# State-space units 1 to 7: loads and output stores issued from POOL's queue in place of SyncE's

## The chip, the cores and the metric

The kernel runs on one core of a Trainium2 chip. The metric is device time in microseconds (us) for one execution; lower is better. Instructions go to engines that run side by side, each in its own order: TensorE (PE in the profile, with its weight loads as PEld), VectorE (DVE), ScalarE (ACT), GpSimd (POOL) and SyncE (SP). SP computes nothing: it issues DMA transfers. POOL can issue DMA transfers too, and computes as well.

## The reference

One layer of a hybrid block in float32: 2048 frames of width 1024. One RMSNorm feeds one input projection, whose columns are split between a state-space layer and chunked attention; both outputs are normalised, joined, projected and added to the input; a SwiGLU feed-forward part and a final RMSNorm follow.

```python
h = rmsnorm(x, norm_mix_g)
proj = h @ w_in
u_ssm, q, k, v = split(proj)                       # 512 columns each
y_ssm = s5_mixer(u_ssm, ...)                       # 32 groups of 16 channels, 64 complex states per group
y_att = chunked_attention(q, k, v, rel_bias)       # 8 heads, own 64-frame chunk and the 8 before it
x = x + concat(rmsnorm(y_ssm), rmsnorm(y_att)) @ w_out
x = x + (silu(h2 @ w_gate) * (h2 @ w_up)) @ w_down # h2 = rmsnorm(x)
return rmsnorm(x)

# inside s5_mixer, per group: bu = B_bar u;  s[t] = lam_bar * s[t-1] + bu[t];  y = Re(C s) + D u
```

## The kernel before

The state-space layer is computed in blocks of eight frames. A first phase writes the input of the layer, u, and three sets of matrices to DRAM: Bst (from the inputs of a block to the state at its end), Tm (from the inputs of a block to its own outputs) and Vm (from the state before a block to its outputs). The recurrence then runs over 256 blocks only.

The work of this layer is cut into eight units (`ssm_unit`, b = 0 to 7, four channel groups each). A unit

1. loads U (eight transfers, one per frame of the block, 16 partitions each), Bst (one), Tm (eight) and Vm (one): 18 transfers, in `load`;
2. multiplies U by Bst on PE (tile `pj`); ACT copies the result to X (line 588);
3. scans X over the blocks on POOL (lines 602 to 605, then the carries in lines 613 and 614);
4. shifts the scanned states by one block into XG, with four transfers from POOL's queue (line 636);
5. multiplies U by Tm and XG by Vm on PE; ACT copies the result to Y (line 646), and eight transfers store Y to DRAM, as `y` (line 649).

U, Bst, Tm and Vm have one buffer each, so a load of the next unit may only land when the matmuls of the unit before that read this buffer are done.

The units run inside the attention phase (`att_phase`). Attention is a list of 128 steps (four blocks of 512 queries, four pairs of heads, two heads, four parts), and units of other work are fed into these steps: the q/k projections, the v projections, the preparation of the next block's input and the eight state-space units, one after the other, each over 15 steps. A unit is a generator; at each step it is advanced so many times, and YL = 8 of these advances lie between the loads and the first matmul, YX = 8 between the XG transfers and the second matmuls.

PE's order is that of the program (every matmul of the attention phase is kept in program order). The order on ACT, DVE, POOL and SP is set by the scheduler when the program is built: by priority, that is place in the program, and by what it expects to be ready. On the chip each engine takes its own list in that order, and an instruction that waits holds all behind it. SP's list holds, beside the transfers of the state-space units: the weights of the projections (`w<-wss`, 1 MB each), their input (`xt`, `raw`), the relative-position bias (`nba`, `nbb`), keys kept from the block before (`k<-ks`, `ks<-k`), halves of q moved to other partitions (`q2h`, `q2l`) and the attention's output (`ya_s<-ya`). POOL's list holds, in this phase, the scans and the XG transfers alone.

Once the last unit is done, the mixing stage loads y (`yr<-y`) and the attention's output, and goes on to the gated unit and the output projection.

`k.ssm_eng`, which is passed to `ssm_unit` as `eng`, is POOL (`nc.gpsimd`).

Of the kernel before, what the change touches and what calls it, by code (L numbers as in the profile page):

```python
# [20 lines left out]
NG, CH, NS = 32, 16, 64  # L21
# [535 lines left out]
def ssm_unit(k, p, psum, S, b, eng):  # L557

    nc = k.nc
    F = GB * CH  # L560
    U = k.t(p, "U", [P, GB, NC])

    def load(out, in_):
        ins = nc.sync.dma_start(out, in_)
        if b == 0:
            k.tc.keep_in_program_order(ins)

    for j in range(L):
        load(U[j * CH : (j + 1) * CH].rearrange("c g (n t) -> c g n t", n=NSB), S["u"].rearrange("(c g) n j t -> c g n j t", c=CH)[:, GB * b : GB * b + GB, :, j])
    gs = slice(GB * b, GB * b + GB)  # L570
    bst = k.t(p, "Bst", [P, GB, P])
    load(bst[:].rearrange("p g m -> p (g m)"), S["bst"][b // 2][:, (b % 2) * GB * P : (b % 2 + 1) * GB * P])
    tm = k.t(p, "Tm", [P, GB, P])
    for i in range(L):
        load(tm[i * CH : (i + 1) * CH], S["kt"].rearrange("c g a m -> c g (a m)")[:, gs, P - CH * i : 2 * P - CH * i])
    vm = k.t(p, "Vm", [P, GB, P])
    load(vm[:], S["v"].rearrange("q g c n m -> (c n) (q g) m")[:, gs, CH:])
    for _ in range(YL):
        yield

    X = k.t(p, "X", [P, 2, GP, NC])
    for q in range(GP):
        ps = k.t(psum, "pj", [P, 2, NC], bufs=2)
        for g2 in range(2):
            k.ta.matmul(ps[:, g2, :], bst[:, 2 * q + g2, :], U[:, 2 * q + g2, :], start=True, stop=True)
        for g2 in range(2):
            for c in range(2):
                nc.scalar.copy(X[g2 * NS : (g2 + 1) * NS, c, q, :], ps[c * NS : (c + 1) * NS, g2, :])
        yield

    a8 = S["a8"]
    qs = slice(GP * b, GP * b + GP)
    Xk = X[:].rearrange("p r q (k s) -> p r q k s", s=8)
    Xe = Xk[:, :, :, :, 7].rearrange("p r q (a b) -> p r q a b", b=8)

    def step(dst, src, e, n):

        ar = a8[:, 0, qs, (0, 7, 15)[e]].unsqueeze(1).to_broadcast([P, 2, GP]).unsqueeze(3).to_broadcast([P, 2, GP, n])
        aw = S["sw"][:, e, :, qs].unsqueeze(3).to_broadcast([P, 2, GP, n])
        t = k.t(p, "st1", [P, 2, GP, NC // 8])  # L600
        t2 = k.t(p, "st2", [P, 2, GP, NC // 8])
        eng.tensor_tensor(t[:, :, :, :n], src, ar, op=ALU.mult)  # L602
        eng.tensor_tensor(t2[:, :, :, :n], src[:, ::-1], aw, op=ALU.mult)
        eng.tensor_tensor(dst, dst, t[:, :, :, :n], op=ALU.add)  # L604
        eng.tensor_tensor(dst, dst, t2[:, :, :, :n], op=ALU.add)  # L605

    def carry(dst, end, i0, n):

        for c in range(2):
            for e in range(2):  # L610
                t = k.t(p, "fx", [P, GP, NC // 8, 7])[:, :, :n]
                pw = a8[:, c if e == 0 else 1 - c, qs, i0 : i0 + 7].unsqueeze(2).to_broadcast([P, GP, n, 7])
                eng.tensor_tensor(t, end[:, e].unsqueeze(3).to_broadcast([P, GP, n, 7]), pw, op=ALU.mult)
                eng.tensor_tensor(dst[:, c], dst[:, c], t, op=ALU.subtract if e == 1 and c == 0 else ALU.add)
            yield

    for s in range(1, 8):
        step(Xk[:, :, :, :, s], Xk[:, :, :, :, s - 1], 0, NC // 8)
        yield
    for b_ in range(1, 8):  # L620
        step(Xe[:, :, :, :, b_], Xe[:, :, :, :, b_ - 1], 1, 4)
        yield
    for a in range(1, 4):
        step(Xe[:, :, :, a : a + 1, 7], Xe[:, :, :, a - 1 : a, 7], 2, 1)
        yield
    yield from carry(Xe[:, :, :, 1:, :7], Xe[:, :, :, :3, 7], 8, 3)
    yield from carry(Xk[:, :, :, 1:, :7], Xk[:, :, :, : NC // 8 - 1, 7], 0, NC // 8 - 1)

    if b == 0:
        k.XG = k.t(p, "XG", [P, GB, NC])  # L630
        nc.gpsimd.memset(k.XG[:, :, 0:1], 0.0)
    XG = k.XG
    XGv = XG[:].rearrange("p (q g) c -> p q g c", g=2)
    for g2 in range(2):
        for c in range(2):
            eng.dma_start(XGv[c * NS : (c + 1) * NS, :, g2, 1:], X[g2 * NS : (g2 + 1) * NS, c, :, : NC - 1])
    for _ in range(YX):
        yield
    Y = k.t(p, "X", [P, GB, NC])
    for q in range(GP):  # L640
        ps = k.t(psum, "pj", [P, 2, NC], bufs=2)
        for g2 in range(2):
            g = 2 * q + g2
            k.ta.matmul(ps[:, g2, :], tm[:, g, :], U[:, g, :], start=True, stop=False)
            k.ta.matmul(ps[:, g2, :], vm[:, g, :], XG[:, g, :], start=False, stop=True)
        nc.scalar.copy(Y[:, 2 * q : 2 * q + 2, :], ps[:])
        if q == GP - 1:
            for j in range(L):
                nc.sync.dma_start(S["y"][b * F : (b + 1) * F, j, :].rearrange("(g c) t -> c g t", c=CH), Y[j * CH : (j + 1) * CH])
        yield  # L650


# [25 lines left out]
def att_phase(k, ident, S, aw, x0, roots):  # L678

    tc, nc, io, pfs = k.tc, k.nc, k.io, k.pfs  # L680
    with ExitStack() as cx:
# [256 lines left out]
        for b in range(NG // GB):  # L938
            units.append(Unit(ssm_unit(k, sp, psum, S, b, k.ssm_eng), SSM_N, 2 + int(SW * b), 2 + int(SW * (b + 1)), light=SL))
# [757 lines left out]
```

## Time and profile before

| | us |
|---|---|
| median of 3 runs | 2290.89 (2288.25 to 2294.39) |
| the profiled execution | 2289.1 |
| its span, first to last instruction | 2287.1 |
| PE busy | 2171.6 |
| DVE busy | 1544.7 |
| ACT busy | 1000.6 |
| POOL busy | 348.7 |

The span runs from the first to the last instruction of the profiled execution. Busy times are sums over an engine's instructions; engines overlap, so they do not add up to the span. DMA transfers are not counted as busy on SP. On POOL their issue is. Where a row of the profile ends in `[1.45 <-DMA ...]`, the engine stood idle for 1.45 us before it, and the named transfer or instruction ended last of what it waited for; a name can be that of another transfer on the same semaphore. "Landing" is the time from the issue of a transfer to its completion.

The first state-space unit loads from 138 us of the span on; the last one stores y at 696 to 700 us.

### The profile page before, as it was taken

To read this page: it belongs to the slowest core of one execution; us is meant where nothing else is said; L and a number is where in the kernel's file an instruction comes from. 1 tells how busy PE (TensorE), PEld (TensorE's weight loads), DVE (VectorE), ACT (ScalarE), POOL (GpSimd) and SP (SyncE) were. 2 spreads that over 40 slices of the span, in tenths; PEclk is the share of its full clock that TensorE was granted. 3 is DMA by queue.
4 is the path that set the end of the run, shared out by engine and by line. 5 is a ranking of instruction groups with operands and counts; after the bars stand their busy time and mean duration, and the time that the engine had idled before them with its cause. 6 is when DMAs were issued, how large, how long until landed. Compare 5 with 4: busy or idle time off the path is not lost.

```text
span 2287.1 us, 30278 instructions
## 1 busy us (share of the span) xinstructions
PE 2171.6 (95%) x10632; PEld 1830.1 (80%) x10632; DVE 1544.7 (68%) x2695; ACT 1000.6 (44%) x1654; POOL 348.7 (15%) x813
## 2 busy tenths in 40 slices
PE   8988899999996899999999999999999989999997
PEld 6777688898985788878888887888888778888886
DVE  7755565555556766876776678666666477789776
ACT  6444555455557652343333335333333343344322
POOL 2245765455660000000000000000000000000000
PEclk9998999999998999999999999999999999999999
DMA  8767886666644534854465567555423297465552
GB/s 299 236 221 220 257 223 201 187 188 179 188 132 124 171 121 147 267 189 151 160 200 178 167 211 258 203 169 188 139 96 110 78 341 252 166 212 193 206 189 74
DMA packets 215256, 428.33 MB, mean 187 GB/s; under 512 B 38592, under 2 KB 61168, under 8 KB 208000
## 3 DMA queue, kind: packets, MB, share of 16 engines
q1 hardware_dynamic: 210368, 412.50, 55.3%
q0 software_dynamic: 4736, 13.91, 2.0%
q8 instruction: 83, 1.36, 0.2%
q14 instruction: 69, 0.57, 0.1%
HBM read 286.86 MB, written 129.00 MB: 182 GB/s over the span
## 4 chain that ended last, share of the span: by engine, by line
PE 80%; DVE 6%; DMA 4%; POOL 4%; issue 3%; ACT 1%; SPq 1%; DVEq 0%; POOLq 0%; ACTq 0%
PE X L79 20%; PE ps L79 19%; PE Y L79 10%; PE pf L79 9%; PE big L79 9%; PE W L79 5%; PE pj L79 4%; PE sc L79 2%; PE pt L82 2%; DMA xt<-in_xp 1%; DMA hd<-wc 1%; POOL X L605 1%; DVE lo L156 1%; POOL X L604 1%; POOL st L602 1%
## 5 line engine op out<-in xcount | busy, mean ns | idle before, releaser
L79 PE MATMUL X<-hi,c 128*128 128x512 f32 x1408 | 451.0, 391 | 6.9 <-DVE c L156 5.4
L79 PE MATMUL ps<-hd,hd 128*128 128x512 f32 (+1 forms) x1968 | 430.8, 381 | 6.1 <-ACT hd L156 4.5
L79 PEld LDWEIGHTS ps<-hd,hd 128*128 128x128 f32 x1968 | 358.0, 189 | 77.7 <-ACT hd L156 5.3
L79 PEld LDWEIGHTS X<-hi,c 128*128 128x128 f32 x1408 | 265.3, 189 | 63.4 <-DVE c L156 6.3
L79 PE MATMUL X<-lo,c 128*128 128x512 f32 x704 | 274.9, 391 | 0.0
L156 ACT CAST hd<-hd 128x1536 fp32r<-128x1536 f32 (+1 forms) x106 | 147.7, 1393 | 236.3 <-DMA hd<-hq 178.7
L79 PE MATMUL Y<-hi,c 128*128 128x512 f32 x704 | 224.7, 390 | 1.5 <-DVE u L1389 1.5
L156 DVE TENSOR_TENSOR hd<-hd 128x1536 fp32r<-128x1536 f32 (+1 forms) x106 | 174.4, 1646 | 29.1 <-ACT hd L156 28.4
L156 DVE TENSOR_TENSOR c<-S,c 128x512 fp32r<-128x512 f32 x176 | 121.0, 689 | 98.3 <-ACT c L156 98.0
L1385 ACT COPY u<-X 128x512 f32<-128x512 f32 x132 | 77.4, 587 | 200.7 <-PE X L79 200.7
L1513 DVE TENSOR_TENSOR acc<-acc,ps 128x512 f32<-128x512 f32 x196 | 130.9, 684 | 50.3 <-PE ps L79 47.8
L156 ACT CAST c<-S 128x512 fp32r<-128x512 f32 x176 | 109.4, 622 | 120.1 <-PE Y L79 61.6
L79 PE MATMUL pf<-hi,w 128*128 128x512 f32 x416 | 153.9, 422 | 8.4 <-ACT w L156 4.7
L79 PE MATMUL big<-m,woh 128*128 128x512 f32 x512 | 161.2, 396 | 0.0
L79 PEld LDWEIGHTS Y<-hi,c 128*128 128x128 f32 x704 | 132.5, 188 | 29.9 <-DVE u L1389 2.2
L79 PEld LDWEIGHTS X<-lo,c 128*128 128x128 f32 x704 | 132.8, 189 | 27.5
L156 ACT CAST c<-raw 128x512 fp32r<-128x512 f32 x132 | 82.3, 623 | 150.5 <-PE Y L79 68.5
L79 PE MATMUL Y<-lo,c 128*128 128x512 f32 x352 | 137.2, 390 | 0.0
L868 DVE TENSOR_TENSOR ptl<-pt,pth 128x640 fp32r<-128x640 f32 (+3 forms) x152 | 98.3, 647 | 47.5 <-ACT pth L867 45.9
L852 ACT ACTIVATE s<-s,mn 128x640 f32<-128x640 f32 (+4 forms) x128 | 98.0, 765 | 65.6 <-DVE mn L849 61.1
L867 ACT CAST pth<-pt 128x640 fp32r<-128x640 f32 (+3 forms) x152 | 83.8, 551 | 95.6 <-PE pt L82 91.5
L79 PE MATMUL W<-hi,c 128*128 128x512 f32 x352 | 115.5, 389 | 0.0
(441 smaller groups left out, 4169.9 us busy)
## 6 DMA issues: line engine op xcount, KB each, us to landing
w<-wss SPq DMA_DIRECT2D x36, 1024.0 KB, 6.0
hq<-g SPq DMA_DIRECT2D x140, 256.0 KB, 2.1
hd<-hq SPq DMA_DIRECT2D x42, 768.0 KB, 4.5
hd<-wc SPq DMA_DIRECT2D x42, 768.0 KB, 6.0
raw<-in_w_gate SPq DMA_DIRECT2D x44, 512.0 KB, 3.8
raw<-in_w_up SPq DMA_DIRECT2D x44, 512.0 KB, 4.3
wc<-px SPq DMA_DIRECT2D x66, 256.0 KB, 3.2
wss<-w SPq DMA_DIRECT2D x12, 1024.0 KB, 5.7
```

What stands on the lines that cost most here:

```text
L79: return self.tc.keep_in_program_order(self.tc.nc.tensor.matmul(*a, **b))
L82: return self.tc.keep_in_program_order(self.tc.nc.tensor.transpose(*a, **b))
L156: return nc.scalar.copy(hi, raw), nc.vector.tensor_tensor(lo, raw, f32(hi), op=ALU.subtract)
L602: eng.tensor_tensor(t[:, :, :, :n], src, ar, op=ALU.mult)
L604: eng.tensor_tensor(dst, dst, t[:, :, :, :n], op=ALU.add)
L605: eng.tensor_tensor(dst, dst, t2[:, :, :, :n], op=ALU.add)
L852: nc.scalar.activation(s[:, :nk], s[:, :nk], AF.Exp, bias=mn[:], scale=-1.0, accum_out=sums[sb, pr][:, hh, qp : qp + 1])
L867: nc.scalar.copy(pth[:, a:b, qp, :], pt[:, a:b, :])
L868: nc.vector.tensor_tensor(ptl[:, a:b, qp, :], pt[:, a:b, :], f32(pth[:, a:b, qp, :]), op=ALU.subtract)
L1385: nc.scalar.copy(u[:], ps[:])
L1513: V.tensor_tensor(a, a, ps[:], op=ALU.add)
```

## The change

In units 1 to 7 the 18 loads are issued from POOL's queue in place of SP's. In the first unit (b = 0) they stay on SP, kept in program order there as before. The eight stores of y are issued from POOL's queue in all eight units. Sizes, tiles and buffers are as before.

```diff
     def load(out, in_):
-        ins = nc.sync.dma_start(out, in_)
         if b == 0:
-            k.tc.keep_in_program_order(ins)
+            k.tc.keep_in_program_order(nc.sync.dma_start(out, in_))
+        else:
+            eng.dma_start(out, in_)
...
         if q == GP - 1:
             for j in range(L):
-                nc.sync.dma_start(S["y"][b * F : (b + 1) * F, j, :].rearrange("(g c) t -> c g t", c=CH), Y[j * CH : (j + 1) * CH])
+                eng.dma_start(S["y"][b * F : (b + 1) * F, j, :].rearrange("(g c) t -> c g t", c=CH), Y[j * CH : (j + 1) * CH])
```

## The prediction

> **What bounds the kernel now.** I read the page's table of engines first, then the waits, the timelines of the stretch in which the state-space units run (130 to 700 us of the span), and the rows of POOL's own DMAs.
>
> ```profile
> PE 2171.6 (95%) x10632; PEld 1830.1 (80%) x10632; DVE 1544.7 (68%) x2695; ACT 1000.6 (44%) x1654; POOL 348.7 (15%) x813
> ```
>
> TensorE is busy for 95% of the span, and its order is fixed, so the end moves only where PE stands still or where its clock drops. POOL has 85% idle. The change touches eight units of about 70 us each. The view of waits over 130 to 710 us (us in total, times, longest) gives the waits that belong to them, and the same view of SP's queue gives one more:
>
> ```profile
> POOL st L602 <- ACT X L588: 217.3, 8, 32.6
> PE pj L79 <- DMA Tm<-kts: 11.1, 4, 3.7
> PE pj L79 <- DMA XG<-X: 3.6, 2, 1.9
> SPq L649 <- ACT X L646: 16.3, 7, 6.1
> ```
>
> The first row is POOL between two units: it stands empty for 217.3/8 = 27 us each time, so there is room for issues. The second is what the change can win or enlarge: PE stands still for 11.1 us in four of the seven handovers from one unit to the next, because the loads of the next unit have not landed when its first matmuls (U by Bst, into pj) come up. The name Tm there is only that of another DMA on the same semaphore; the matmul reads U and Bst. PE's timeline at the seven handovers, units 1 to 7 in order (start, us, what, in brackets PE's idle time before it):
>
> ```profile
> 227.11 0.67 PE L79 MATMUL pj<-U,Bst 128*128 128x256 f32 x2 [1.45 <-DMA Tm<-kts]
> 300.02 1.35 PE L79 MATMUL pj<-U,Bst 128*128 128x256 f32 x5 [2.92 <-DMA Tm<-kts]
> 364.46 1.97 PE L79 MATMUL pj<-U,Bst 128*128 128x256 f32 x8 [3.00 <-DMA Tm<-kts]
> 441.04 1.24 PE L79 MATMUL pj<-U,Bst 128*128 128x256 f32 x5
> 504.94 1.89 PE L79 MATMUL pj<-U,Bst 128*128 128x256 f32 x8
> 575.05 1.89 PE L79 MATMUL pj<-U,Bst 128*128 128x256 f32 x8
> 642.56 1.88 PE L79 MATMUL pj<-U,Bst 128*128 128x256 f32 x5 [3.73 <-DMA Tm<-kts]
> ```
>
> PE was ready at start minus idle: 225.66, 297.10, 361.46, 441.04, 504.94, 575.05, 638.83. What starts each handover is ACT's second copy of Y; its rows for the same seven handovers:
>
> ```profile
> 215.86 0.58 ACT L646 COPY X<-pj 128x512 f32<-128x512 f32 x1
> 284.96 0.59 ACT L646 COPY X<-pj 128x512 f32<-128x512 f32 x1 [1.10 <-PE pj L79]
> 352.35 0.59 ACT L646 COPY X<-pj 128x512 f32<-128x512 f32 x1 [1.09 <-PE pj L79]
> 426.71 0.59 ACT L646 COPY X<-pj 128x512 f32<-128x512 f32 x1 [0.92 <-PE pj L79]
> 493.48 0.59 ACT L646 COPY X<-pj 128x512 f32<-128x512 f32 x1 [0.92 <-PE pj L79]
> 563.02 0.59 ACT L646 COPY X<-pj 128x512 f32<-128x512 f32 x1 [1.10 <-PE pj L79]
> 629.39 0.59 ACT L646 COPY X<-pj 128x512 f32<-128x512 f32 x1 [1.10 <-PE pj L79]
> ```
>
> The copies end at 216.44, 285.55, 352.94, 427.30, 494.07, 563.61 and 629.98. Then SP issues eight stores of y and eight loads of U, one behind the other. SP's timeline at units 1, 2, 3 and 7:
>
> ```profile
> 216.47 4.16 SPq L649 DMA_DIRECT2D y<-X  x8
> 220.72 3.81 SPq L564 DMA_DIRECT2D U<-u  x8
> ...
> 285.58 3.61 SPq L649 DMA_DIRECT2D y<-X  x8
> 291.21 0.34 SPq L695 DMA_DIRECT2D w<-wss  x1
> 291.59 3.53 SPq L564 DMA_DIRECT2D U<-u  x7
> ...
> 351.92 0.32 SPq L564 DMA_DIRECT2D U<-u  x1
> 352.96 4.96 SPq L649 DMA_DIRECT2D y<-X  x8
> 357.97 3.62 SPq L564 DMA_DIRECT2D U<-u  x7
> ...
> 632.08 3.94 SPq L649 DMA_DIRECT2D y<-X  x8
> 636.52 3.53 SPq L564 DMA_DIRECT2D U<-u  x7
> ```
>
> At units 1, 3 and 7 PE starts 2.58, 2.87 and 2.51 us after the last U issue ends (224.53, 361.59, 640.05). At unit 2 a 1 MB weight load stood ahead on SP: it held the queue from 289.19 to 291.21, and U landed only 4.9 us after its last issue (295.12). At unit 7 the queue was 2.1 us late (632.08 against 629.98). So on SP the chain is copy of Y, eight stores, eight loads, landing, and twice something foreign in between.
>
> **The change, part by part.**
>
> *Taken from SP.* For units 1 to 7 the 18 loads, and for all eight units the 8 stores: 7 x 18 + 8 x 8 = 190 issues. At unit 1 the sixteen that stand ahead of the matmul cost 224.53 - 216.47 = 8.06 us. SP is not on the path elsewhere in these stretches, so I count only what comes earlier through it: the weight load at unit 2 and the 2.1 us at unit 7. These leave the chain.
>
> *Put on POOL's queue.* POOL's present DMAs, by form (busy us, mean ns):
>
> ```profile
> L636 POOL DMA_DIRECT2D XG<-X x32 | 19.7, 616 | 2.4 <-POOL X L614 2.4
> L368 POOL DMA_DIRECT2D vs<-v x16 | 10.1, 636 | 10.8 <-DVE v L288 7.6 <-DVE ny L113 1.7 <-DVE nv L109 1.6
> L358 POOL DMA_DIRECT2D kts<-kt x4 | 2.2, 547 | 8.3 <-DVE kt L357 7.2 <-DVE nf L111 1.0
> ```
>
> A store of y and a load of Tm touch 16 partitions in 64 runs, and are nearest to the kts row (16 partitions, 64 KB): 0.55 us. A load of U has 256 runs like the vs row: 0.63 us. I take one U load ahead of the stores, as at 351.92 above (its buffer is free once the matmuls that read it end, some 1.4 us before the copy does). From the end of the copy to the end of the last U issue: 8 x 0.55 + 7 x 0.63 = 8.81 us. On SP it was 8.09, 9.57, 8.65 and 10.07 us at units 1, 2, 3 and 7.
>
> *Landing.* No row shows a load of this kind on POOL's queue. The tile views give the times from issue to landing (min/median/max), first of XG (POOL, 127.5 KB), then of U and of y (both SP, 64 KB):
>
> ```profile
> DMA to landing us min/median/max: 2.4/4.6/7.9
> DMA to landing us min/median/max: 2.2/3.0/7.5
> DMA to landing us min/median/max: 2.0/2.1/7.4
> ```
>
> At their shortest the two queues differ by 0.2 to 0.4 us, with twice the bytes on POOL's side; at their medians by 1.6. XG is issued among large weight loads, so I take the short end: 2.6 us after the last issue, as at units 1, 3 and 7. The long end, 1.6 more, goes into the range.
>
> *Stalls after.* Copy end + 8.81 + 2.6 gives landings at 227.85, 296.96, 364.35, 438.71, 505.48, 575.02 and 641.39. Against PE's ready times that leaves stalls of 2.2, 0, 2.9, 0, 0.5, 0 and 2.6 us: 8.2 in place of 1.45 + 2.92 + 3.00 + 3.73 = 11.1. Gain 2.9 us.
>
> *Clock.* Around the longest stall (unit 7) and after that of unit 3, the windows view (width, busy PE, PEld, DVE, ACT, POOL, granted clock, DMA share, GB/s):
>
> ```profile
> 643.00:647.00 4.00, 4.00 (x14) 3.40 (x13) 0.21 (x1) 2.68 (x8) 0.00 (x0) 0.57 0.53 136
> 365.00:369.00 4.00, 3.81 (x21) 3.27 (x20) 0.83 (x2) 3.24 (x9) 0.24 (x1) 1.00 0.77 224
> 575.00:645.00 70.00, 66.27 (x410) 60.25 (x410) 35.28 (x64) 37.05 (x75) 35.01 (x88) 0.99 0.63 180
> ```
>
> After 3.73 us of idle the granted clock was 0.57 for 4 us, after 3.00 us it stayed at 1.00. So a stall above some 3.0 to 3.7 us costs 4 x 0.43 = 1.7 us more, and at 2.6 us unit 7 saves it. The Trainium skill (TensorE: Matmul & The Clock Gate, Part 1) puts the idle window at about 3.4 us; these two rows agree with it.
>
> *POOL's own work behind the issues.* In POOL's order the 8 loads of Tm and one of Vm stand between U and the scan: 8 x 0.55 + 0.63 = 5.0 us, one more for Bst, 5.6. The scan cannot start before U has landed, the matmuls have run and ACT has copied eight times; at unit 3, ACT's timeline has
>
> ```profile
> 365.64 3.04 ACT L588 COPY X<-pj 64x256 f32<-64x256 f32 x8 [4.51 <-issue]
> ```
>
> which ends at 368.68, 4.2 us after PE's start at 364.46. With the landing of 2.6 that is 6.8 us against 5.6: hidden, with 1.2 us of cover. If the cover goes, each microsecond costs one at the units where PE already waits for XG (3.6 us in two waits above). A load of Bst, whose buffer is free early, may stand between two scan steps, 0.6 us; I count 1.5 us for two or three units. Who waits behind POOL's queue: only this kernel's scan; nothing else uses POOL here.
>
> *The last unit.* Its y goes to the mixing stage, which loads it after other transfers; with 8 x 0.55 in place of 3.6 us the store is under 1 us later, and I count nothing.
>
> Sum: -2.9 - 1.7 + 1.5 = -3.1 us. The profiled execution took 2289.1 us (span 2287.1), 1.8 below the median of 2290.9; less 3.1 it is 2286.0, and on the median's footing 2287.8. I forecast 2288 us, which is within 0.3% (6.9 us, about what a measurement of this kernel can tell from no change).
>
> **The rivals.**
>
> *POOL's issues are slow beside VectorE (slower).* DVE is busy for 35.28 of 70 us in the row above. If each of the sixteen issues ahead of the matmul waits for half of a DVE operation of 0.7 us at half occupancy, that is 16 x 0.35 x 0.5 = 2.8 us; the long landing alone is 1.6. With 1.6 to 2.8 us more at every handover the stalls become 3.8, 1.5, 4.5, 0, 2.1, 1.6, 4.2 = 17.7 up to 5.0, 2.7, 5.7, 0.5, 3.3, 2.8, 5.4 = 25.4; less 11.1, and with two to three more clock drops (3.4 to 5.1 us), the time is 10 to 19 us longer, with Bst's 1.5 some 2302 to 2312. It decides from 0.8 us per handover on, where unit 7 crosses the clock's limit again. For it speaks that no load of 256-byte runs was ever on this queue; against it, that the 32 XG issues in these same stretches took 0.587 to 0.694 us (mean 0.616, row above). The Trainium skill (SBUF — State Buffer, SBUF: two separate sides) warns of just this: POOL writes its descriptors through a port that some VectorE operations lock, with an issue of 620 ns becoming 3100 ns. The XG rows do not show it. Chance 0.31.
>
> *The queues come apart (faster).* If POOL gets more U loads out ahead of the stores, or its landing is as short as 2.4 us, every handover's stall goes: -11.1 - 1.7 = -12.8, some 2278; the attention's transfers, no longer behind 26 issues, can add to it. One stall that could go so stands in PE's timeline, where hi is made from a load on SP's queue:
>
> ```profile
> 252.30 0.50 PE L79 MATMUL pf<-hi,w 128*128 128x512 f32 x1 [3.15 <-ACT hi L728]
> ```
>
> With it 2275. Against it: POOL is no quicker per issue than SP. Chance 0.27.
>
> *The cover on POOL goes (slower by little).* If the 5.6 us of Tm, Vm and Bst outlast the 6.8, the scan starts 1 to 2 us late. XG is already awaited in two units; if it decides in three or four, that is 3 to 8 us on top of the forecast: 2291 to 2296. Chance 0.08.
>
> **How the numbers follow.** The forecast has 0.34; its own range is 2282 to 2295 (unit 2's landing of 4.9 us, one or no U load ahead). Of it 0.05 lies below -0.3% and 0.04 above +0.3%. The first rival gives 0.27 slower and 0.04 same, the second 0.25 faster and 0.02 same, the third 0.04 and 0.04. Together faster 0.30, same 0.35, slower 0.35. The range that leaves out some 2 in 10 runs from 2274 to 2310.
>
> **What would show it.** Right: POOL's rows have 190 more DMA issues of 0.53 to 0.65 us; POOL's wait for ACT's copy falls from 217 us by some 100; PE's wait before U by Bst is 7 to 10 us in total, none at unit 2; the clock row at unit 7 is 1.00. Wrong: POOL DMA rows of 1 us or more, U's landing above 4 us, waits before U by Bst of more than 15 us, or PE waiting for XG by more than 5 us. If all of these fit and the time is off by over 0.3%, then the order of SP's remaining transfers changed the attention's stalls, which I have not counted.

## The result, and the profile after

The changed kernel takes 2319.95 us in the median of four runs (2313.49 to 2325.72), against 2291.39 us for the kernel before in the runs beside it. The ratio is 1.0126 with a 95% interval of 1.0106 to 1.0146: 1.3% slower, 28.6 us. The forecast was 2288 us with a range of 2274 to 2310, so the time lies above the range, on the side of the first rival but beyond it. The profiled execution of after is the slowest of the four: 2325.72 us, span 2323.8 us, 36.7 us more than the span of before.

The page's table of engines, after:

```profile
PE 2186.9 (94%) x10632; PEld 1842.6 (79%) x10632; DVE 1546.9 (67%) x2695; ACT 999.4 (43%) x1654; POOL 450.0 (19%) x1003
```

POOL has its 190 more instructions, as the change says, and 101 us more of busy time. PE does the same 10,632 matmuls but is busy 15 us longer: the same work at a lower clock. The next view tells how much of the loss lies in the state-space stretch. It is the windows view between the same two matmuls of PE's fixed order, in before and then in after (start and end, width, then busy us and count of PE, PEld, DVE, ACT and POOL, granted clock, DMA share, GB/s):

```profile
150.16:706.50 556.34, 507.64 (x3033) 454.03 (x3032) 319.59 (x603) 301.13 (x638) 300.21 (x704) 0.96 0.67 195
```

```profile
148.60:736.35 587.75, 516.28 (x3034) 460.63 (x3032) 320.87 (x603) 300.01 (x638) 401.63 (x894) 0.93 0.63 185
...
232.00:236.00 4.00, 3.56 (x9) 2.88 (x10) 1.04 (x2) 1.45 (x4) 1.71 (x3) 0.50 1.04 279
```

The same work takes 31.4 us longer. Of that 8.6 is PE's busy time, at a granted clock of 0.93 in place of 0.96, and the rest, (587.75 - 516.28) - (556.34 - 507.64) = 22.8 us, is PE standing still. The last row is 4 us around the end of the first stall: the clock is at 0.50. The waits of after over the units (us, times, longest) say where PE stands:

```profile
PE pj L79 <- DMA Tm<-kts: 35.4, 6, 8.0
...
POOL st L603 <- ACT X L589: 25.7, 8, 4.1
...
PE pj L79 <- DMA XG<-X: 6.0, 2, 5.0
```

PE's wait before U by Bst grew from 11.1 us in four handovers to 35.4 us in six, by 24.3 us, which is about the idle time gained. The wait for XG grew by 2.4. PE's timeline at the seven handovers:

```profile
232.44 3.75 PE L79 MATMUL pj<-U,Bst 128*128 128x256 f32 x8 [8.03 <-DMA Tm<-kts]
313.24 3.64 PE L79 MATMUL pj<-U,Bst 128*128 128x256 f32 x8 [6.99 <-DMA Tm<-kts]
382.56 3.75 PE L79 MATMUL pj<-U,Bst 128*128 128x256 f32 x8 [6.58 <-DMA Tm<-kts]
459.42 1.89 PE L79 MATMUL pj<-U,Bst 128*128 128x256 f32 x8
528.18 3.68 PE L79 MATMUL pj<-U,Bst 128*128 128x256 f32 x8 [4.64 <-DMA Tm<-kts]
601.74 1.97 PE L79 MATMUL pj<-U,Bst 128*128 128x256 f32 x8 [1.53 <-DMA Tm<-kts]
673.32 3.75 PE L79 MATMUL pj<-U,Bst 128*128 128x256 f32 x8 [7.64 <-DMA Tm<-kts]
```

After each of the five stalls of 4.6 us and more the eight matmuls take some 3.7 us, where they take 1.89 with no stall: half the clock. POOL's issues, by form, were not the reason (busy, mean ns):

```profile
L650 POOL DMA_DIRECT2D y<-X x64 | 32.3, 513 | 14.8 <-ACT X L647 13.0 <-DMA U<-u 1.8
L567 POOL DMA_DIRECT2D U<-u x56 | 31.5, 568 | 78.9 <-PE pj L79 71.8 <-DMA y<-X 3.7 <-issue 3.3
```

They are a little shorter than forecast. What is long is the time from the issue to the landing. POOL's timeline of after at units 1 and 2, and two rows of unit 5:

```profile
214.25 4.04 POOL L650 DMA_DIRECT2D y<-X  x8 [0.46 <-ACT X L647]
218.67 0.57 POOL L567 DMA_DIRECT2D U<-u  x1 [0.38 <-DMA y<-X]
219.98 3.33 POOL L567 DMA_DIRECT2D U<-u  x6 [0.74 <-DMA y<-X]
...
295.00 4.04 POOL L650 DMA_DIRECT2D y<-X  x8 [0.45 <-ACT X L647]
299.02 1.12 POOL L567 DMA_DIRECT2D U<-u  x2
301.67 2.79 POOL L567 DMA_DIRECT2D U<-u  x5 [1.52 <-issue]
...
518.11 0.51 POOL L650 DMA_DIRECT2D y<-X  x1 [1.78 <-DMA U<-u]
...
523.53 0.56 POOL L567 DMA_DIRECT2D U<-u  x1 [1.58 <-issue]
```

At units 1 and 2 the last U issue ends at 223.31 and 304.46; PE starts 9.1 and 8.8 us later, not 2.6. SP's timeline of after at the same two handovers, and then SP's at unit 1 of before, from the last two U loads on:

```profile
219.57 0.33 SPq L701 DMA_DIRECT2D wss<-w  x1
219.99 0.38 SPq L696 DMA_DIRECT2D w<-wss  x1
...
300.37 1.76 SPq L696 DMA_DIRECT2D w<-wss  x2
```

```profile
223.60 0.94 SPq L564 DMA_DIRECT2D U<-u  x2
224.58 3.73 SPq L564 DMA_DIRECT2D Tm<-kts  x8
...
229.90 0.41 SPq L695 DMA_DIRECT2D w<-wss  x1
```

In before the 1 MB weight load stands on SP behind U and Tm and goes out at 229.90, after PE has started. In after it goes out between the stores and the last U loads, with a 1 MB store ahead of it at unit 1 and a second load behind it at unit 2. At units 3, 6 and 7 a weight load goes out beside the U loads too (376.01, 593.72 and 662.43), at units 4 and 5 the last one goes out 3.3 us before the first U load. Unit 5's stall of 4.64 us comes otherwise: POOL's queue stood for 1.78 us before the last store, until the first U load had landed, and for 1.58 us, with no releaser, before the last U load, which then took 4.6 us to land.

### The profile page after: what moved, and what is told of

Same layout as the page of the kernel before. It is cut to its first block, busy times and chain, and to the rows that moved or that the text cites. A ratio compares the mean times of both kernels' runs of the same rounds, so it can differ in the third digit from the quotient of the medians.

```text
span 2323.8 us, 30354 instructions
## 1 busy us (share of the span) xinstructions
PE 2186.9 (94%) x10632; PEld 1842.6 (79%) x10632; DVE 1546.9 (67%) x2695; ACT 999.4 (43%) x1654; POOL 450.0 (19%) x1003
## 4 chain that ended last, share of the span: by engine, by line
PE 78%; POOL 7%; DMA 6%; DVE 4%; issue 2%; ACT 2%; SPq 0%; DVEq 0%; POOLq 0%; ACTq 0%
PE X L79 20%; PE ps L79 19%; PE Y L79 10%; PE big L79 9%; PE pf L79 7%; PE W L79 5%; PE pj L79 4%; PE sc L79 2%; DMA Tm<-kts 1%; PE pt L82 1%; DMA xt<-in_xp 1%; POOL X L605 1%; POOL X L606 1%; POOL st L603 1%; POOL fx L614 1%
## 5 line engine op out<-in xcount | busy, mean ns | idle before, releaser
L1390 DVE TENSOR_TENSOR u<-u,Y 128x512 f32<-128x512 f32 x88 | 60.4, 687 | 83.1 <-ACT u L1386 60.5
```

Source lines behind the costliest of these rows:

```text
L1390: V.tensor_tensor(u[:], u[:], ps[:], op=ALU.add)
```

## Theories

- **T1**: SP, freed of 26 issues per unit, sends its 1 MB transfers into the handover, and U, on another queue, comes behind them.
- **T2**: POOL's queue lands its transfers late by itself.
- **T3**: VectorE's operations hold up POOL's writing of descriptors.
- **T4**: U stands behind eight stores on POOL's one queue, and so comes too late.

Where T1 and T4 are set against each other, T1 means that SP's being free matters, and T4 that U's lateness does. In all kernels of the layer below PE's order is that of before; the orders on ACT and DVE are told where they matter.

## Experiments

**Transfers alone.** A program of its own, without the layer: eight rounds, three times over, each closed by two small VectorE operations that read some of what was loaded:

```text
A  U on POOL                     E  2 x 1 MB on SP, then U on ACT
B  2 x 1 MB on SP, U on POOL     F  2 x 1 MB in 256 KB pieces on SP, U on POOL
C  2 x 1 MB, then U, on SP       G  8 copies 128x2048 on VectorE, U on POOL
D  U, then 2 x 1 MB, on SP       H  U on SP
```

> Leaves out the layer's computation: it measures transfers alone. Eight loads of U (64 KB each, 256-byte runs) stand on POOL's, SP's or ACT's queue, alone or beside two 1 MB loads of 8192-byte rows on SP. T1 (large transfers of SP's queue are served ahead of POOL's queue): alone on POOL (A) the last U lands 2 to 3 us after its issue; with the two 1 MB loads ahead on SP (B) 6 us or more, in four pieces of 2 KB rows (F) less; U on SP ahead of the 1 MB loads (D) as alone. T2 (POOL's queue is slow by itself): A lands 5 us or more after its issue, and H (on SP alone) 2 to 3. T3 (VectorE's copies hold POOL's writing of descriptors): G, beside copies on VectorE, takes 1 us or more per issue or lands later than A; T1 expects G as A.

The transfers' view (count, KB each, median us to landing) in windows around one round each, in the order H, A, B, C, D, E, F:

```profile
U<-in_u SPq DMA_DIRECT2D x8, 64.0 KB, 2.6
...
U<-in_u POOLq DMA_DIRECT2D x8, 64.0 KB, 2.9
...
U<-in_u POOLq DMA_DIRECT2D x8, 64.0 KB, 8.7
...
U<-in_u SPq DMA_DIRECT2D x8, 64.0 KB, 7.6
...
U<-in_u SPq DMA_DIRECT2D x8, 64.0 KB, 2.9
...
U<-in_u ACTq DMA_DIRECT2D x8, 64.0 KB, 6.6
...
U<-in_u POOLq DMA_DIRECT2D x8, 64.0 KB, 8.5
```

Alone, U lands in 2.6 us on SP and 2.9 on POOL: T2 falls. Behind two 1 MB loads it lands in 6.6 to 8.7 us, on whichever queue it stands. Ahead of them it is as if alone. Cutting the large loads into pieces, which T1 expected to help, did not: a miss. The Trainium skill (DMA: Bandwidth & Descriptors, Issuing engines are not separate DMA queues) says that transfers from all issuing engines run on the same 16 DMA engines and that a second issuing engine saves only issue time; B, C and E agree.

Round G did not run as meant: VectorE made its copies at the start of the span, beside the first round A. That round tells T3's size all the same (groups by form, in the first round A and in the second):

```profile
L62 DVE COPY V<-V 128x2048 f32<-128x2048 f32 x10 | 12.2, 1220 | 0.3
L31 POOL DMA_DIRECT2D U<-in_u x8 | 9.7, 1226 | 8.3 <-DVE U L21 8.3
```

```profile
L31 POOL DMA_DIRECT2D U<-in_u x8 | 4.4, 563 | 9.2 <-DVE T L35 9.2
```

Beside copies of 1.22 us POOL issues one load per copy, in 1.23 us in place of 0.56. T3 exists, then, but not in this kernel, where POOL's U issues took 0.568 us and y's 0.513.

**The weight loads held back.** The kernel after, units' loads emitted one step earlier, and the next two weight loads after a unit's U loads wait for U through a small transfer:

```diff
+    if b:
+        k.after = [U, U]
...
+                if k.after:
+                    nc.sync.dma_start(f32(w[:, 0, 0:1]), k.after.pop()[:, 0, 0:1])
                 nc.sync.dma_start(f32(w[:]), S["ws"][n])
```

> The kernel after, with the unit's loads emitted one step earlier and the next two 1 MB weight loads behind a unit's loads held on SP until the last U has landed; nothing is left out. T1 (the freed SP queue sends the 1 MB weight loads into the handover, and U waits behind them): U lands 2.5 to 4 us after its last issue at every handover, PE's wait for U by Bst falls from 35 us to 12 or less, and the time to 2286 to 2298. T2 (POOL's queue is slow by itself): waits and time stay as after, 2312 to 2325. T4 (stores and loads one behind the other on POOL are the cost): 2305 to 2320.

2335.37 us, ratio 1.0179 (1.0162 to 1.0196). Its waits:

```profile
PE pf L79 <- DMA w<-wss: 41.0, 3, 16.4
...
PE pj L79 <- DMA Tm<-kts: 6.6, 2, 4.0
```

U's landing is where T1 put it (median 3.0 us; at unit 2, where after had up to 9.5, all eight landed in 2.7 to 3.1), and the wait before U by Bst falls to 6.6 us, and 0.8 more under U's name. The time does not follow, and lies far above T1's 2286 to 2298: loads held back at three handovers were themselves needed soon, and PE waits 41.0 us for them. What delays U is shown; that the hold is a remedy is refuted.

**Its control**, the kernel after with the loads emitted one step earlier and no hold (`Unit(..., 1 if b else 0, ...)`):

> The kernel after, with the loads of units 1 to 7 emitted one step earlier, as in the kernel that held the weights, but without that hold: its control. T1: the landings of U and PE's waits come back, 25 to 40 us of waits for U by Bst, time 2310 to 2326. If waits stay under 12 us, the earlier place in the program and not the hold had taken them away.

One time, 2329.57 us, 4 us above T1's range; waits before U by Bst of 38.9 us, in two rows of 25.0 and 13.9. As after: it was the hold, not the place in the program, that shortened the landings.

**The two halves.** The loads alone on POOL, stores back on SP:

```diff
-                eng.dma_start(S["y"][...], Y[...])
+                nc.sync.dma_start(S["y"][...], Y[...])
```

> Loads on POOL, stores on SP: half of the change. T4 (the stores ahead of the loads on one queue are the cost): the U loads go out 4 us earlier, stalls go, 2280 to 2290. T1: SP's weight loads are held back only by the eight stores, so some handovers still meet them: 2290 to 2308. T2: landing 5 to 9 us, but from an issue 4 us earlier: 2288 to 2298.

2289.42 us, ratio 0.9979 (0.9963 to 0.9995). And the stores alone on POOL, all loads on SP:

```diff
-        else:
-            eng.dma_start(out, in_)
+        else:
+            nc.sync.dma_start(out, in_)
```

> Stores on POOL, loads on SP: the other half. T1: on SP the weight loads stay behind U, U goes out some 4 us earlier than before, so PE's wait for U by Bst falls from 11 us to 3 or less: 2274 to 2286. T2: the loads are on SP, so as fast: 2274 to 2290. T4: the same. If it is slower than 2300, stores on POOL are the cost by themselves and T1 is wrong.

2286.04 us, ratio 0.9971 (0.9958 to 0.9983), with orders on ACT and DVE the same as before. Waits before U by Bst are 2.5 us with the loads alone, and 3.0 + 1.2 (the second under U's name) with the stores alone. So neither half costs anything, each gains a little, and both together lose 1.3%. The loads alone gain less than the waits for U that they remove, 11.1 to 2.5 us: in their profile PE has a new wait of 13.9 us for VectorE, which itself waits 12.5 us for `xt`, an input that SP issues at 226.72, behind the stores of y and a 1 MB store; before and after do not have it. With the loads alone ACT's order is that of after and DVE's differs in two instructions: what separates 2289 from 2320 us is on which queue the eight stores stand. That is the upper end of T4's time and just below the lower end of T1's, so one more kernel was needed.

**Stores on both queues.** Loads on POOL; y stored from SP, and once more from POOL into an array that nobody reads:

```diff
             for j in range(L):
-                eng.dma_start(S["y"][...], Y[...])
+                eng.dma_start(S["y2"][...], Y[...])
+                nc.sync.dma_start(S["y"][...], Y[...])
```

> Loads on POOL; the stores of y are issued twice, from SP as in the kernel before (to y) and from POOL as in the kernel after (to a second array that nobody reads; this adds 512 KB of stores per unit). On SP it is the kernel with the loads alone moved, which had no waits for U; on POOL it is the kernel after, where U stands behind eight stores. PE's and ACT's orders are those of both. If SP's stores, by holding the weight loads back, are what keeps U's landing short: waits for U of 10 us or less, 2285 to 2300. If U's place behind POOL's stores is what makes it meet the weight loads, which come some 5 us after the copy of Y whatever SP does before: last issue of U 9 us after the copy, landing 5 to 9 us where a weight load stands beside it, waits of 25 to 40 us, 2308 to 2325.

2332.23 us, ratio 1.0190 (1.0161 to 1.0219), 7 us above the second case's range. Unit 2 with the loads alone, POOL's timeline and SP's:

```profile
293.30 3.93 POOL L567 DMA_DIRECT2D U<-u  x7 [17.57 <-PE pj L79]
298.38 0.56 POOL L567 DMA_DIRECT2D U<-u  x1 [1.15 <-issue]
```

```profile
294.08 3.61 SPq L650 DMA_DIRECT2D y<-X  x8
299.72 1.78 SPq L696 DMA_DIRECT2D w<-wss  x2
```

The same with stores on both, and its waits:

```profile
296.30 4.04 POOL L650 DMA_DIRECT2D y<-X  x8 [0.45 <-ACT X L647]
300.33 1.13 POOL L567 DMA_DIRECT2D U<-u  x2
303.11 2.79 POOL L567 DMA_DIRECT2D U<-u  x5 [1.65 <-issue]
```

```profile
296.04 4.61 SPq L651 DMA_DIRECT2D y<-X  x8
301.68 1.78 SPq L697 DMA_DIRECT2D w<-wss  x2
```

```profile
PE pj L79 <- DMA Tm<-kts: 19.6, 3, 7.7
...
PE pj L79 <- DMA U<-u: 9.0, 3, 5.8
```

ACT's order is that of after in both, and SP does the same: its stores start with the copy of Y, and two weight loads follow 5.6 us after the first store. In the first kernel all eight U loads are issued before them, the last by 298.94; in the second five are issued between 303.11 and 305.90, behind them, and PE waits 7.7 us there and 28.6 in all. So SP's stores do not protect U. U's place behind POOL's stores makes it late, T4, and what it is then late for is T1's weight loads, which come some 5 us after the copy even when SP has the stores. The wait of 28.6 us is the second case's; the time holds more, for PE waits 14.5 us for VectorE as well, as with the loads alone.

**The reverse.** The kernel before, with the loads `w<-wss` alone on POOL:

```diff
-                nc.sync.dma_start(f32(w[:]), S["ws"][n])
+                nc.gpsimd.dma_start(f32(w[:]), S["ws"][n])
```

> The kernel before, with the units' loads and stores all on SP as they were; only the 1 MB loads w<-wss (blocks of queries 1 to 3) go to POOL's queue. Nothing is left out. T1: the weight loads no longer stand behind stores and loads of SP's queue and meet U as in the kernel after: U on SP lands 5 to 9 us after its last issue at two or more handovers, PE's wait for U by Bst grows from 11 to 18 us or more, time 2296 to 2320. If POOL's own scans hold the weight loads back, PE waits for w in their place. T2 or T4 (POOL's queue, or its stores, are the cost): U lands as before, time 2286 to 2296.

2386.64 us, ratio 1.0409 (1.0369 to 1.0448). With every unit's transfer on SP as before, the wait before U by Bst doubles:

```profile
PE pf L79 <- DMA w<-wss: 62.0, 10, 17.0
PE pj L79 <- DMA Tm<-kts: 21.5, 6, 7.4
...
305.95 0.53 POOL L695 DMA_DIRECT2D w<-wss  x1 [21.47 <-PE pf L79]
```

The last row is POOL's timeline at unit 2: the weight load goes out among the U loads, which SP issues from 303.71 to 308.44, and U lands up to 9.1 us after its issue. So what protected U in before is that U and the weight loads shared a queue. This kernel's orders on ACT and DVE are not those of before, and its time lies far above T1's 2296 to 2320: most of the 4% is another cost, the 62.0 us that PE waits for the weights themselves.

**U early beside a free SP.** Both kernels take U out of the stores' way and leave SP free. One puts the eight stores behind the next unit's U loads on POOL, the other puts them on ACT (in the first the last unit, which has no next, stores at once):

```diff
+            k.store = store
...
+    if b:
+        k.store()
...
-                eng.dma_start(S["y"][...], Y[...])
+                nc.scalar.dma_start(S["y"][...], Y[...])
```

> The kernel after, with loads and stores both on POOL, but the eight stores of y of a unit stand behind the eight U loads of the next unit in POOL's queue. Nothing protects U from SP's weight loads. T4 (issued behind eight stores, U is out too late to be ahead of the weight loads; going 4.5 us earlier is enough): last U issue 4 to 4.5 us earlier against the copy of Y, PE's wait for U by Bst 35 us to under 8, time 2276 to 2292. T1 alone (whatever the order on POOL, the free SP queue meets U): U still lands 5 us or more after its last issue at units 1, 2 and 7, waits of 12 to 20 us, time 2295 to 2310.

> Loads on POOL as in the kernel after, the eight stores of y on ACT's queue: SP is as free as after, but the U loads no longer stand behind stores. If being early is enough: last U issue about 4 us after the copy of Y, U's landing 3 to 5 us, PE's wait for U by Bst under 6 us; ACT is held for some 3.5 us by its stores at each handover; time 2282 to 2300. If only SP's queue held by stores or loads protects U (T1 alone): waits for U of 15 us or more and 2305 to 2320.

Waits before U by Bst: 2.2 us in all and none. Times: 2333.69 us, ratio 1.0185 (1.0154 to 1.0216), and 2327.24 us, 1.0154 (1.0137 to 1.0171). U was cured and the time was not; both misses on the time. In the first the built program has another order on ACT, with the copies of X later, and in the second ACT itself is held by the stores. The waits of the first on PE, and of the second on ACT, show it:

```profile
PE pj L79 <- ACT X L591: 18.2, 5, 4.3
...
PE pj L79 <- DMA XG<-X: 13.6, 3, 7.3
```

```profile
ACT s L853 <- DMA y<-X: 27.0, 6, 6.4
```

That these account for the whole of the 42 and 35 us is not shown.

**Versions.** U and Bst on SP, the rest on POOL (`late` is set for Tm and Vm); U alone on POOL (`u` is set for the eight U loads); and, with queues as in the second half or as before, the loads emitted one step earlier:

```diff
+            (eng if late else nc.sync).dma_start(out, in_)
...
+            (eng if u else nc.sync).dma_start(out, in_)
...
-            units.append(Unit(..., 2 + int(SW * (b + 1)), light=SL))
+            units.append(Unit(..., 2 + int(SW * (b + 1)), 1 if b else 0, light=SL))
```

> Only U and Bst, which the first matmuls need, stay on SP; the eight loads of Tm, Vm and the eight stores of y are on POOL. T1: weight loads stand behind U on SP, U goes out beside the stores: PE's wait for U by Bst 6 us or less, time 2276 to 2286, as with the stores alone moved or some 2 us better. If POOL's added 5 us of issues hold up the scan, PE's wait for XG grows above 5 us and the time is 2288 to 2296.

2295.37 us, ratio 1.0009 (0.9992 to 1.0027): the wait for XG is 10.4 us in three waits, so wait and time are those of its second case. That POOL's issues cause the wait is not shown: with all loads on POOL and the stores on SP it is 1.0 us, and in the next kernel, with only U on POOL, 7.6. At unit 2 a weight load still stood ahead of U on SP (waits before U by Bst: 4.5 us there, 7.5 in all).

> Of units 1 to 7 only the eight U loads are issued from POOL's queue; stores, Bst, Tm and Vm stay on SP. U goes out beside the stores, and POOL has 4.5 us of issues instead of 10 to 15 per handover, none between U and the scan. T1: PE's wait for U by Bst 4 us or less, wait for XG 4 us or less, time 2276 to 2288. If the weight loads now meet U at more handovers than with all loads moved (SP has 10 issues fewer ahead of them): 2290 to 2300.

2285.15 us, ratio 0.9975 (0.9963 to 0.9987): waits before U by Bst 0.1 us, as expected, for XG 7.6 where 4 or less was expected.

> Stores on POOL, loads on SP and emitted one step earlier in the program, so that U and not the weight load comes first on SP at unit 2. T1: PE's wait for U by Bst 2 us or less (3 to 4 with the stores alone moved), time 2274 to 2286. If it is no faster than with the stores alone moved, the place in the program does not set SP's order at that handover.

2285.45 us, ratio 0.9970 (0.9958 to 0.9982): no wait before U by Bst, XG 4.1. At unit 2 all eight U loads now go out on SP ahead of the weight load (281.48 to 285.32, the weight load at 290.51), so the place in the program does set SP's order there; the time does not show it. This kernel, the stores alone moved (0.9971) and U alone moved (0.9975) cannot be told apart, and are the fastest seen: some 0.3% below the kernel before.

> The kernel before with the loads of units 1 to 7 emitted one step earlier; queues as before. T1: U stays behind the eight stores on SP, so its last issue is where it was; only the weight load ahead of U at unit 2 can go, 3 us: PE's wait for U by Bst 8 to 11 us, time 2284 to 2293.

2292.84 us, ratio 1.0002 (0.9990 to 1.0014): waits of 5.2 + 2.4 us, 3.5 less than before, and no change of the time that can be told.

## Why the prediction was wrong

- **What bounds the kernel.** Right: nearly all of the difference within the units is PE's wait before U by Bst and the clock after it.
- **POOL's issues.** Right: 0.55 and 0.63 us were forecast, 0.513 and 0.568 measured, one U ahead of the stores as assumed. From the first store to the end of the last U issue it took 9.1 and 9.5 us at units 1 and 2, and 11.3 at unit 5 with its two gaps; 8.81 was forecast from the copy's end.
- **Landing.** This step failed. I took "the short end: 2.6 us after the last issue", and 4.2 for the long one; at units 1 and 2 PE starts 9.1 and 8.8 us after it, and at no handover at which it waits less than 4.1. The terms of the sum behind it went with it: stalls of 35.4 us where 8.2 were forecast, five of them long enough for the clock.
- **Why it failed.** The step before: "SP is not on the path elsewhere in these stretches, so I count only what comes earlier through it". I let the foreign transfers at units 2 and 7 leave the chain with SP. But SP's order was what kept 1 MB loads behind U, and the row of unit 2 in before, 4.9 us of landing behind one such load, was the price of losing it; after loses it at units 1, 2, 3, 6 and 7. I quoted that row and read it as a delay that the change removes.
- **Clock.** That a stall can cost clock was right, the sign wrong: no stall saved, five long ones, the granted clock at 0.50 to 0.57 in the 4 us from the end of each, and 8.6 us more of busy PE. The limit of 3.0 to 3.7 us does not hold even in before, where it was read from two rows: the clock was 0.58 in the 4 us after 2.09 us of idle (394.02 to 398.02) and 0.50 after 3.09 (541.73 to 545.73). The idle window that the Trainium skill gives (TensorE: Matmul & The Clock Gate, Part 1) fits the runs of eight in after, of which none was slowed at 1.53 us of idle and all were at 4.64 and above; the 2.09 us are less than this window, and the clock fell all the same.
- **Cover on POOL.** It held: POOL still waits for ACT's copies before the scan, 25.7 us in eight waits, and XG's wait grew by 2.4 us, near the 1.5 counted for Bst, though no run shows that Bst's issue makes it. So the third rival is out.
- **First rival.** Right in sign, wrong in mechanism: issues did not slow beside VectorE. The port lock that the Trainium skill tells of (SBUF — State Buffer, SBUF: two separate sides) fits what was seen beside 1.22 us copies, 1.23 us per issue in place of 0.56, less than the 3100 ns quoted in the prediction; it does not show in this kernel's issue times.
- **Second rival.** Its short stalls came with either half alone, where U goes out beside the stores, and not its price: 7 to 9 us less of waits for U gained 3 to 7 us, to 2289 and 2286 us, where 2275 to 2278 was forecast.
- **The last unit.** Counted at nothing, and the traces agree: behind the stretch above PE stands still for 48.0 us in after and 48.2 in before. Of the profiled 36.7 us, 5.3 lie outside the stretch; behind it PE is busy 7.1 us longer, at a granted clock of 0.98 in place of 0.99. Whether the change has to do with that clock is not shown.

## What to carry to other kernels

Before moving transfers off a queue, list what remains on it and ask what its order kept behind the moved ones: a queue that looks like a bottleneck can be the only thing that holds large transfers behind small urgent ones. Moving half of a chain so that it goes out beside the other half gained 0.2 to 0.3%; moving the whole chain kept its length and lost its place, at 1.3%. Size a landing from the row in which the same transfer stood behind a large one, if anything large can get ahead of it.

## What was not expected of the hardware

- 64 KB loads behind two 1 MB loads land in 6.6 to 8.7 us on each of three queues, 2.6 to 2.9 alone; pieces of 256 KB instead of 1 MB made no difference (8.5 against 8.7).
- Eight such loads from POOL beside back-to-back VectorE copies of 1.22 us: 1.23 us per issue instead of 0.56. Why this kernel's VectorE work does not do that was not tried.
- POOL's issues showed gaps with no releaser of 1.15 to 1.65 us among the U loads at unit 2, in three kernels. Their cause is open.
- The length of one stall of PE did not settle whether the clock fell: in before 2.09 us of idle were followed by a granted clock of 0.58, and 2.92 and 3.00 us (units 2 and 3) by 1.00, each over 4 us.
